# One trunk kernel on one core: addresses of the weight slots, the queue of the general expert path, and the shape of the down products

## The chip, the cores and the metric

The kernel runs on one core of one Trainium2 chip. The metric is the device time of one execution in microseconds (us). The core has five instruction queues that matter here: TensorE (PE, matrix products, with its weight loads shown apart as PEld), VectorE (DVE), ScalarE (ACT), GpSimd (POOL) and SyncE (SP, which here does nothing but start DMAs), and 16 DMA engines that bring weights from HBM into SBUF. Each queue executes its instructions in the order in which they were issued; queues wait for each other through semaphores.

## The reference, cut to what matters

There are 256 tokens of 1024 channels and two layers. Each layer mixes tokens (layer 0 by windowed means, layer 1 by latent attention) and then runs a hierarchical mixture of experts: 4 groups of 8 experts, each token goes to the two best experts of its best group. All numbers are float32.

```python
def hier_moe(h, rg_w, rg_b, re_w, re_b, w_gate, w_up, w_down):
    ...
    gp = jax.nn.softmax((ht @ rg_w + rg_b).astype(jnp.float32), axis=-1)
    g_idx = jnp.argmax(gp, axis=-1)
    ...
    top_p, top_i = lax.top_k(jax.nn.softmax(el, axis=-1), TOP_K)
    gates = g_prob[:, None] * top_p / jnp.sum(top_p, axis=-1, keepdims=True)
    ...
    def expert_block(args):
        xr, e = args
        return (jax.nn.silu(xr @ w_gate[e]) * (xr @ w_up[e])) @ w_down[e]
    ...
    out = jnp.zeros((T, D), jnp.float32).at[row_tok].add(y * row_w[:, None])
```

The 32 experts of a layer have 6 MB of weights each, gate and up 1024 x 512 and down 512 x 1024, and all of them are read whatever the routing says: 192 MB per layer, nearly all of the 419 MB that the kernel moves.

## The kernel before

**Weights and slots.** The host packs all weights into chunks of 1 MB, 128 partitions of 2048 floats. `order` (lines 90 to 95) is the list of chunks as they are needed: one for the pooling mixer, 16 pairs of experts in layer 0 with 12 chunks a pair, 11 for attention, 16 pairs in layer 1. SBUF holds 22 slots of one chunk each (`slot`, line 100). `load` (line 103) takes the next chunk of the list and issues its DMA on SP's queue (line 110). `done` (line 116) says that a chunk has been used, and issues the next load into the slot that comes free; that DMA waits on SP for the last product that reads the slot. So the list is fetched in order, up to 22 chunks ahead.

**Routing.** `route_half` transposes a block of 128 tokens on PE. `route_block` is a generator in three stages. Stage 1 sums the squares, takes `rstd` (two GpSimd operations in `rsqrt`, lines 162 and 163), adds the residual to the output sums with an identity product (line 323), and lets ScalarE form `xh`, the upper part of the normalised tokens. Stage 2 is the router product (line 331). Stage 3 finds the group and the two experts with a chain of small DVE operations (lines 334 to 348, ending in the mask `mb`), forms the lower part `xl` of the tokens with two GpSimd operations per half (lines 351 and 353), and calls `gates`. `route_end` counts tokens per expert with small products against the masks, gives each token its place `pos` (line 381), builds selection matrices `sel` (`prepare`, line 404), sets `flag` when an expert has more than 64 tokens, and gathers the tokens of the first four experts by products with `sel` (`gather`, lines 422 and 424). `warm` issues products whose result isn't used.

**The general path.** `overflow` (lines 529 to 566) is for the case that an expert has more than 64 tokens. All queues read `flag` (line 532) and branch on it (lines 537 and 538); inside is a loop over the 16 pairs whose weight loads are on SP's queue (line 543). It stands at the head of `experts`, so each queue reaches the branch in front of the first pair.

**Experts.** `experts` takes the pairs in order. Two experts share the partitions of PE's output, 64 each (`CAP`). Eight chunks hold gate and up (line 468, products of 512 columns into the PSUM banks `g` and `u`); ACT and DVE form the activation `sg`, PE transposes it (line 486) into `hT`. Four chunks hold the down weights, chunk c the output columns 256c to 256c + 255 with all four 128-row blocks of both experts. Per chunk c, PE makes eight products of 256 columns (line 507), ACT and DVE take the result to SBUF in two float32r parts (lines 511 and 512), and `scatter` adds them with the transposed selection into the sums `acc[c]` (line 497): one PSUM bank per c, with the two token blocks in its halves. The scatter of one chunk is issued behind the products of the next. The last pair of a stage also evicts the sums and starts the following part (`during`).

A float32 product shows as two matmul instructions and two weight loads.

Of the kernel before, what the change touches and what calls it, by code (L numbers as in the profile page):

```python
# [19 lines left out]
P = 128  # L20
# [7 lines left out]
NE = 32  # L28
# [23 lines left out]
def trunk(ctx: ExitStack, tc: tile.TileContext, x_d, w_d, small_d, rows_d, out_d):  # L52
# [102 lines left out]
    V.memset(ones_bf, 1.0)  # L155
    zero_bf = cst.tile([P, P], BF16, name="zero_bf")
    V.memset(zero_bf, 0.0)
    match = cst.tile([P, 2, 8], F32, name="match")
# [122 lines left out]
    def route_start(l):  # L281
        r = Route()
        r.l = l
        r.ss, r.xT = [None] * 2, [None] * 2
        r.rstd = sb([P, 2], f"rstd{l}")
        r.lg = sb([P, 2, 40], "lg")
        r.g8 = sb([P, 2, 8], "g8")
        r.e8 = sb([P, 2, 8], "e8")
        r.el = sb([P, 2, NE], "el")
        r.mb = sb([P, 2, NE], "mb", dt=BF16)  # L290
        r.gw = sb([P, 2, NE], "gw")
        r.pos = sb([P, 2, NE], "pos")

        r.acc = [ps("c") for _ in range(NB)]
        return r

    def warm(n):

        p = ps("u")
        for _ in range(n):  # L300
            T.matmul(p, zero_bf, zero_bf[:, 0:1].to_broadcast([P, 512]), start=True, stop=True)

# [13 lines left out]
    def route_block(r, i):  # L316
# [3 lines left out]
        rsqrt(r.rstd[:, i:i + 1], r.ss[i][:, 0:1], 1.0 / D)  # L320

        for c in range(NB):
            T.matmul(r.acc[c][:, i * 256:(i + 1) * 256], ident, x(i, c * 256, 256),
                     start=i == 0, stop=False, skip_group_check=True)
        for hh in range(2):
            A.mul(xh[:, i, hh * 512:(hh + 1) * 512], xs[i][hh], r.rstd[:, i:i + 1])
        yield
        p = ps("t")
        for k in range(DC):
            c = C_RW + 288 * l + 36 * k  # L330
            T.matmul(p[:, 0:40], r.xT[i][:, k // 4, k % 4 * P:(k % 4 + 1) * P], small[:, c:c + 40], start=k == 0, stop=k == DC - 1)
        yield
        lg, g8, e8, el = r.lg[:, i], r.g8[:, i], r.e8[:, i], r.el[:, i]
# [11 lines left out]
        V.tensor_copy(match[:, 1, 0:2], e8[:, 0:2])  # L345
        t32 = sb([P, NE], "t32")
        V.match_replace(t32, match[:, 1], el, HIT)
        V.tensor_scalar(r.mb[:, i], t32, HIT, None, op0=OP.is_ge)
        for hh in range(2):
# [3 lines left out]
            G.tensor_tensor(xs[i][hh], xx, xh[:, i, hh * 512:(hh + 1) * 512].bitcast(F32), op=OP.subtract)  # L353
        gates(r, i)
        yield

    def gates(r, i):
        nm = sb([P, 2], "nm", bufs=2)
        V.tensor_scalar(nm[:, 0:1], r.e8[:, i, 0:1], -1.0, None, op0=OP.mult)
        V.tensor_scalar(nm[:, 1:2], r.g8[:, i, 0:1], -1.0, None, op0=OP.mult)  # L360
        ex = sb([P, NE], "ex")
# [90 lines left out]
    def experts(r, before_last, during):  # L452
# [4 lines left out]
        for q in range(NPAIR):  # L457
# [35 lines left out]

            def scatter(c, ys=ys, selT=h.selT[:, j], last=last):
                for i in range(2):
                    for n in range(2):
                        T.matmul(r.acc[c][:, i * 256:(i + 1) * 256], selT[:, i], ys[c][:, n], start=False,  # L497
                                 stop=last and n == 1, skip_group_check=True)
                if last:
                    for i in range(2):  # L500
                        evac(c + i, x(i, c * 256, 256), r.acc[c][:, i * 256:(i + 1) * 256])

            for c in range(NB):
                w = chunk(base + 8 + c)
                p = ps("t")
                for f, e in by_expert(base + 8 + c, 4):
                    T.matmul(p[e * CAP:(e + 1) * CAP, 0:256], hT[:, f, e * CAP:(e + 1) * CAP],  # L507
                             w[:, e * 1024 + f * 256:e * 1024 + f * 256 + 256], start=f == 0, stop=f == 3)
                done(base + 8 + c)
                y = sb([P, 2, 256], "y", "b2", dt=F32R)  # L510
                A.copy(y[:, 0], p[:, 0:256])  # L511
                V.tensor_tensor(y[:, 1], p[:, 0:256], y[:, 0].bitcast(F32), op=OP.subtract)  # L512
                ys.append(y)
                if c:
                    scatter(c - 1)
                if last:
                    during(c)
            if last:
                scatter(NB - 1)
                for c in range(NB, NB + 4):  # L520
                    during(c)
            else:
                pend = lambda scatter=scatter: scatter(NB - 1)
            if q == NPAIR - 2:
# [4 lines left out]
    def overflow(r):  # L529

        l = r.l
        v = nc.values_load(r.flag[0:1, 0:1], min_val=0, max_val=1)
        hks = sb([P, 2, P], "hks", "b1")
        w, hs, hT = (sb([P, 512], n, "b2") for n in ("wov", "hso", "hTo"))
        gate = sb([P, 2, 2], "gate")
        g, u, pt = ps("g"), ps("u"), ps("t")
        with tc.If(v > 0):
            with tc.For_i(0, NPAIR, 1) as q:
                V.tensor_copy(gate, r.go[:, :, ds(q * 2, 2)])

                def weights(k, e, n):
                    o = e * 1024 + n * 512
                    nc.sync.dma_start(w, w_d[ds(MOE_CHUNK[l] + k + q * 12, 1), :, o:o + 512].rearrange("o p n -> (o p) n"))

                for e in range(2):
                    for i in range(2):
                        for k in range(DC):
                            for t in (upper_x, x):
                                T.matmul(pt[:, 0:P], t(i, k * P, P).bitcast(F32), ident, start=t is upper_x, stop=t is x)
                            hk = hks[:, k % 2]  # L550
                            V.tensor_scalar(hk, pt[:, 0:P], small[:, C_FFN + 8 * l + k:C_FFN + 8 * l + k + 1], None,
                                            op0=OP.mult)
                            for n, p in enumerate((g, u)):
                                weights(k, e, n)
                                T.matmul(p, hk, w, start=k == 0, stop=k == DC - 1)
                        A.activation(hs, g, AF.Silu)
                        V.scalar_tensor_tensor(hs, hs, gate[:, i, e:e + 1], u, op0=OP.mult, op1=OP.mult)
                        for f in range(4):
                            T.transpose(pt[:, f * P:(f + 1) * P], hs[:, f * P:(f + 1) * P], ident)
                        A.copy(hT, pt)  # L560
                        for c in range(NB):
                            for f in range(4):
                                if f % 2 == 0:
                                    weights(8 + c, e, f // 2)
                                T.matmul(r.acc[c][:, i * 256:(i + 1) * 256], hT[:, f * P:(f + 1) * P],
                                         w[:, f % 2 * 256:(f % 2 + 1) * 256], start=False, stop=False, skip_group_check=True)

# [121 lines left out]
    def attention():  # L689
# [219 lines left out]
        for n in range(4):  # L909
# [40 lines left out]
    stages = [route_block(r, i) for i in range(2)]  # L950
    for _ in range(3):
        for stage in stages:
            next(stage)
    route_end(r)
# [25 lines left out]
def packed(v):  # L980
# [3 lines left out]
    for l in range(2):  # L984
        c = w[MOE_CHUNK[l]:MOE_CHUNK[l] + NPAIR * 12].reshape(NPAIR, 12, P, 2, 2, 512)
        for n, name in enumerate(("w_gate", "w_up")):
            c[:, 0:8, :, :, n] = v[name][l].reshape(NPAIR, 2, 8, P, 512).transpose(0, 2, 3, 1, 4)
        d = w[MOE_CHUNK[l]:MOE_CHUNK[l] + NPAIR * 12].reshape(NPAIR, 12, P, 2, 4, 256)
        d[:, 8:12] = v["w_down"][l].reshape(NPAIR, 2, 4, P, NB, 256).transpose(0, 4, 3, 1, 2, 5)
    a = w[ATT_CHUNK:]  # L990
# [53 lines left out]
```

## Time and profile before

| | us |
|---|---|
| median of 3 runs | 1082.19 |
| lowest and highest | 1081.85, 1083.34 |
| the profiled execution | 1082.35 |
| its span in the trace | 1080.3 |
| PE busy | 1007.9 (93%) |
| DVE, ACT, POOL busy | 255.4, 165.2, 85.1 |

The profile is of one execution. Its times count from the first instruction of the program; the span ends with the last one, and the execution's own time holds 2.05 us more around it. A matmul's end is modelled, so a busy PE isn't a PE at its peak. A row of the timeline has start, duration, engine, line and operation, and in brackets the idle time ahead of it and what ended that. The first expert stage lies between 56 and 508 us, attention and the second routing behind it, the second expert stage between 628 and 1070 us.

### The profile page before, as it was taken

To read this page: it belongs to the slowest core of one execution; us is meant where nothing else is said; L and a number is where in the kernel's file an instruction comes from. 1 tells how busy PE (TensorE), PEld (TensorE's weight loads), DVE (VectorE), ACT (ScalarE), POOL (GpSimd) and SP (SyncE) were. 2 spreads that over 40 slices of the span, in tenths; PEclk is the share of its full clock that TensorE was granted. 3 is DMA by queue.
4 is the path that set the end of the run, shared out by engine and by line. 5 is a ranking of instruction groups with operands and counts; after the bars stand their busy time and mean duration, and the time that the engine had idled before them with its cause. 6 is when DMAs were issued, how large, how long until landed. Compare 5 with 4: busy or idle time off the path is not lost. (4 is left out here: it accounts for less than half of the span.)

```text
span 1080.3 us, 15133 instructions
## 1 busy us (share of the span) xinstructions
PE 1007.9 (93%) x6338; PEld 574.3 (53%) x6338; DVE 255.4 (24%) x543; ACT 165.2 (15%) x413; POOL 85.1 (8%) x88
## 2 busy tenths in 40 slices
PE   6699999999999998989889889999999999999996
PEld 5545555555555543535878645555555555554543
DVE  5502121212121201123775512121212121211102
ACT  4100101010101010024632200101010101010013
POOL 4400000000000000000464400000000000000001
PEclk9889999999999999999999999999999999999999
DMA  9989999999999999999655959999999999999993
GB/s 361 417 352 420 419 418 421 418 419 421 417 419 419 419 420 419 420 420 418 241 229 175 370 224 420 420 418 420 419 419 419 418 420 420 417 420 420 417 417 148
DMA packets 59260, 418.86 MB, mean 388 GB/s; under 512 B 6704, under 2 KB 6704, under 8 KB 9136
## 3 DMA queue, kind: packets, MB, share of 16 engines
q1 hardware_dynamic: 58608, 416.84, 93.7%
q8 instruction: 53, 0.87, 0.3%
q10 hardware_dynamic: 576, 0.96, 0.3%
q14 instruction: 23, 0.19, 0.0%
HBM read 416.72 MB, written 1.05 MB: 387 GB/s over the span
## 5 line engine op out<-in xcount | busy, mean ns | idle before, releaser
L468 PE MATMUL ps_g<-slot,xg 128*64 128x512 f32 x1024 | 274.9, 604 | 24.2 <-DMA slot<-w_in 14.9
L468 PE MATMUL ps_u<-slot,xg 128*64 128x512 f32 x1024 | 270.7, 595 | 0.0
L507 PE MATMUL ps_t<-slot,hT 128*64 128x256 f32 x2048 | 245.1, 384 | 9.2 <-DVE hT L221 8.3
L507 PEld LDWEIGHTS ps_t<-slot,hT 128*64 128x64 f32 x2048 | 140.8, 137 | 84.6 <-DVE hT L221 12.1
L468 PEld LDWEIGHTS ps_u<-slot,xg 128*64 128x64 f32 x1024 | 84.4, 138 | 138.0 <-issue 138.0
L468 PEld LDWEIGHTS ps_g<-slot,xg 128*64 128x64 f32 x1024 | 76.5, 137 | 148.1 <-issue 97.3
L477 DVE SCALAR_TENSOR_TENSOR sg<-sg,gates,ps_u 128x512 f32<-128x512 f32 x32 | 23.9, 747 | 473.1 <-PE ps_u L468 473.1
L512 DVE TENSOR_TENSOR y<-ps_t,y 128x256 fp32r<-128x256 f32 x128 | 54.3, 424 | 242.9 <-ACT y L511 242.9
L497 PEld LDWEIGHTS ps_c<-y,selT 128*128 128x128 f32 x512 | 68.4, 188 | 61.5 <-issue 36.9
L497 PE MATMUL ps_c<-y,selT 128*128 128x256 f32 x512 | 94.5, 306 | 0.1
L511 ACT CAST y<-ps_t 128x256 fp32r<-128x256 f32 x128 | 47.6, 372 | 248.9 <-PE ps_t L507 248.9
L476 ACT ACTIVATE sg<-ps_g 128x512 f32<-128x512 f32 x32 | 19.1, 597 | 409.2 <-PE ps_g L468 393.0
L422 PE MATMUL ps_t<-sel,xh 128*128 128x256 f32 x256 | 54.3, 294 | 0.0
L422 PE MATMUL ps_t<-sel,xl 128*128 128x256 f32 x256 | 52.3, 286 | 0.0
L424 DVE TENSOR_TENSOR xg<-ps_t,small 128x512 f32<-128x512 f32 x64 | 44.2, 691 | 28.7 <-PE ps_t L422 28.7
L422 PEld LDWEIGHTS ps_t<-sel,xh 128*128 128x128 f32 x256 | 40.8, 196 | 1.3 <-issue 1.1
L422 PEld LDWEIGHTS ps_t<-sel,xl 128*128 128x128 f32 x256 | 40.7, 195 | 0.0
L944 POOL TENSOR_TENSOR x<-x,slot 128x256 f32<-128x256 f32 x5 | 3.5, 724 | 450.5 <-ACT junka L942 450.5
L162 POOL TENSOR_SCALAR rstd_a<-acca 128x2 f32<-128x2 f32 x1 | 0.2, 192 | 473.8 <-DVE acca L655 473.8
L619 POOL TENSOR_TENSOR slot<-slot 128x1024 fp32r<-128x1024 f32 x11 | 27.1, 2485 | 3.8 <-PE ps_c L191 3.4
L219 ACT COPY hT<-ps_g 128x256 f32<-128x256 f32 x32 | 11.9, 372 | 64.9 <-DVE hT L221 61.3
L486 PE MATMUL ps_g<-ident,sg 128*128 128x128 f32 x128 | 19.8, 277 | 1.3 <-DVE sg L477 1.3
(263 smaller groups left out, 678.3 us busy)
## 6 DMA issues: line engine op xcount, KB each, us to landing
slot<-w_in SPq DMA_DIRECT2D x391, 1024.0 KB, 19.9
slot<-w_in SPq DMA_DIRECT2D x10, 512.0 KB, 13.3
x<-x_in SPq DMA_DIRECT2D x4, 256.0 KB, 5.4
out<-x SPq DMA_DIRECT2D x2, 256.0 KB, 2.6
out<-x ACTq DMA_DIRECT2D x2, 256.0 KB, 2.6
small<-small_in ACTq DMA_DIRECT2D x1, 388.5 KB, 4.2
rb<-rows_in ACTq DMA_DIRECT2D x1, 40.0 KB, 5.7
```

The costliest lines, as they stand in the source:

```text
L219: A.copy(dst, src)
L422: T.matmul(o, w(i, kk * P, P), h.sel[:, i], start=n == 0, stop=n == 3)
L424: V.tensor_tensor(h.xg[hh][:, 2 * m:2 * m + 2], p.rearrange("p (k s) -> p k s", k=2), small[:, c:c + 2, None].to_broadcast([P, 2, 4 * CAP] ...
L468: T.matmul((g, u)[n][e * CAP:(e + 1) * CAP], h.xg[k // 4][:, k % 4, s0 + e * CAP:s0 + (e + 1) * CAP], w[:, e * 1024 + n * 512:e * 1024 + n ...
L476: A.activation(sg, g, AF.Silu)
L477: V.scalar_tensor_tensor(sg, sg, h.gate[:, j:j + 1], u, op0=OP.mult, op1=OP.mult)
L486: T.transpose(pt[:, f * P:(f + 1) * P], sg[:, f * P:(f + 1) * P], ident)
L497: T.matmul(r.acc[c][:, i * 256:(i + 1) * 256], selT[:, i], ys[c][:, n], start=False, stop=last and n == 1, skip_group_check=True)
L507: T.matmul(p[e * CAP:(e + 1) * CAP, 0:256], hT[:, f, e * CAP:(e + 1) * CAP], w[:, e * 1024 + f * 256:e * 1024 + f * 256 + 256], start=f == ...
L511: A.copy(y[:, 0], p[:, 0:256])
L512: V.tensor_tensor(y[:, 1], p[:, 0:256], y[:, 0].bitcast(F32), op=OP.subtract)
L619: eng.tensor_tensor(lo, w, hi.bitcast(F32), op=OP.subtract)
```

## The change

- **Down products.** Except in the last pair of a stage, the four down chunks of a pair are packed anew: output half n (512 columns) takes chunks 8 + 2n and 9 + 2n, each with two of the four row blocks of both experts. PE makes products of 512 columns, eight calls per chunk become four, and the result is taken to SBUF in two operations of 512 columns per half.
- **Sums.** They are held as `acc[i][hh]`, by token block i and half hh of the columns, one bank each. The identity product of the residual is two calls of 512 columns per block instead of four of 256. `scatter` adds 512 columns at once, the first half's behind the first chunk of the second half, the second half's in the next pair.
- **Routing order.** The router product stands ahead of the identity product. The lower part of the tokens moves out of `route_block` into `lower_x` and from four GpSimd operations per block to two DVE operations. `gates` moves out of `route_block` into `route_end`, behind `prepare`.
- **General path.** Its weight loads go to GpSimd's queue. The loops are now over pair and expert, once for all pairs but the last and once for the last, whose down chunks keep the old packing; the two token parts are added on DVE in front of the transpose.
- **SBUF.** GpSimd's DMAs need scratch memory, which lies at the start of SBUF and grows from 16 to 512 bytes per partition. All tiles behind it move, the slots with them. To make room, `zero_bf` goes (`warm` uses `tri`) and `t32` and `ex` share a buffer.

```diff
-        for c in range(NB):
-            T.matmul(r.acc[c][:, i * 256:(i + 1) * 256], ident, x(i, c * 256, 256),
-                     start=i == 0, stop=False, skip_group_check=True)
-        for hh in range(2):
-            A.mul(xh[:, i, hh * 512:(hh + 1) * 512], xs[i][hh], r.rstd[:, i:i + 1])
-        yield
         p = ps("t")
         for k in range(DC):
...
+        for hh in range(2):
+            A.mul(xh[:, i, hh * 512:(hh + 1) * 512], xs[i][hh], r.rstd[:, i:i + 1])
+
+        for hh in range(2):
+            T.matmul(r.acc[i][hh], ident, xs[i][hh], start=True, stop=False, skip_group_check=True)
         yield
...
+    def lower_x(r, i):
+
         for hh in range(2):
             xx = xs[i][hh]
-            G.tensor_scalar(xx, xx, r.rstd[:, i:i + 1], None, op0=OP.mult)
             xs[i][hh] = tokens("xl", F32R)
-            G.tensor_tensor(xs[i][hh], xx, xh[:, i, hh * 512:(hh + 1) * 512].bitcast(F32), op=OP.subtract)
-        gates(r, i)
-        yield
+            V.scalar_tensor_tensor(xs[i][hh], xx, r.rstd[:, i:i + 1], xh[:, i, hh * 512:(hh + 1) * 512].bitcast(F32),
+                                   op0=OP.mult, op1=OP.subtract)
...
         r.first = prepare(r, 0)
+        for i in range(2):
+            gates(r, i)
...
+                for n in range(2):
+                    p = ps("t")
+                    for f in range(4):
+                        w = chunk(base + 8 + 2 * n + f // 2)
+                        for e in range(2):
+                            o = e * 1024 + f % 2 * 512
+                            T.matmul(p[e * CAP:(e + 1) * CAP], hT[:, f, e * CAP:(e + 1) * CAP], w[:, o:o + 512],
+                                     start=f == 0, stop=f == 3)
+                        if f % 2:
+                            done(base + 8 + 2 * n + f // 2)
+                            if n == 1 and f == 1:
+                                scatter(0, 512)
+                    ys += [two_parts(p, 512), None]
+                pend = lambda scatter=scatter: scatter(2, 512)
...
-                    nc.sync.dma_start(w, w_d[ds(MOE_CHUNK[l] + k + q * 12, 1), :, o:o + 512].rearrange("o p n -> (o p) n"))
...
+                        G.dma_start(w, w_d[ds(MOE_CHUNK[l] + k + q * 12, 1), :, ds(e * 1024 + n * 512, 512)]
+                                    .rearrange("o p n -> (o p) n"))
...
         out_proj(1, [ps("g"), ps("u")], {(0, 0): lambda: next(stages), (0, 1): lambda: next(stages),
-                                         (0, 3): lambda: next(stages), (1, 2): lambda: route_half(r, 1, 0)})
+                                         (0, 3): lambda: lower_x(r, 0), (1, 2): lambda: route_half(r, 1, 0)})
         route_half(r, 1, 1)
         list(route_block(r, 1))
+        lower_x(r, 1)
         route_end(r)
...
-    nc = bacc.Bacc("TRN2", target_bir_lowering=False, num_devices=1, dynamic_dma_scratch_size=16)
+    nc = bacc.Bacc("TRN2", target_bir_lowering=False, num_devices=1, dynamic_dma_scratch_size=512)
```

More of the change, by code (lines that the diff above doesn't have):

```diff
@@ L155, in trunk @@
     V.memset(ones_bf, 1.0)
-    zero_bf = cst.tile([P, P], BF16, name="zero_bf")
-    V.memset(zero_bf, 0.0)
     match = cst.tile([P, 2, 8], F32, name="match")
@@ L292, in route_start @@
         r.pos = sb([P, 2, NE], "pos")
-        r.acc = [ps("c") for _ in range(NB)]
+        r.acc = [[ps("c") for _ in range(2)] for _ in range(2)]
         return r
@@ L300, in warm @@
         for _ in range(n):
-            T.matmul(p, zero_bf, zero_bf[:, 0:1].to_broadcast([P, 512]), start=True, stop=True)
+            T.matmul(p, tri, tri[:, 0:1].to_broadcast([P, 512]), start=True, stop=True)
     def route_half(r, i, hh):
@@ L360, in gates @@
         V.tensor_scalar(nm[:, 1:2], r.g8[:, i, 0:1], -1.0, None, op0=OP.mult)
-        ex = sb([P, NE], "ex")
+        ex = sb([P, NE], "ex", "row", 1)
         A.activation(ex, r.el[:, i], AF.Exp, bias=nm[:, 0:1])
@@ L492, in experts, with scatter @@
             ys = []
-            def scatter(c, ys=ys, selT=h.selT[:, j], last=last):
+            def scatter(c, n, ys=ys, selT=h.selT[:, j], last=last):
                 for i in range(2):
-                    for n in range(2):
-                        T.matmul(r.acc[c][:, i * 256:(i + 1) * 256], selT[:, i], ys[c][:, n], start=False,
-                                 stop=last and n == 1, skip_group_check=True)
+                    o = r.acc[i][c // 2][:, c % 2 * 256:c % 2 * 256 + n]
+                    for m, y in enumerate(ys[c]):
+                        T.matmul(o, selT[:, i], y, start=False, stop=last and m == 1, skip_group_check=True)
@@ L499, in scatter @@
                 if last:
                     for i in range(2):
[L501 to L516, printed above, removed]
+                        evac(c + i, x(i, c * 256, 256), r.acc[i][c // 2][:, c % 2 * 256:(c % 2 + 1) * 256])
@@ new lines, in two_parts @@
+            def two_parts(p, n):
+                hi, lo = (sb([P, n], "y", "b2", dt=F32R) for _ in range(2))
+                A.copy(hi, p)
+                V.tensor_tensor(lo, p, hi.bitcast(F32), op=OP.subtract)
+                return hi, lo
+            if last:
+                for c in range(NB):
+                    w = chunk(base + 8 + c)
+                    p = ps("t")
+                    for f, e in by_expert(base + 8 + c, 4):
+                        T.matmul(p[e * CAP:(e + 1) * CAP, 0:256], hT[:, f, e * CAP:(e + 1) * CAP],
+                                 w[:, e * 1024 + f * 256:e * 1024 + f * 256 + 256], start=f == 0, stop=f == 3)
+                    done(base + 8 + c)
+                    ys.append(two_parts(p[:, 0:256], 256))
+                    if c:
+                        scatter(c - 1, 256)
@@ L517, in experts @@
                     during(c)
-            if last:
-                scatter(NB - 1)
+                scatter(NB - 1, 256)
                 for c in range(NB, NB + 4):
@@ L532, in overflow, with weights @@
         v = nc.values_load(r.flag[0:1, 0:1], min_val=0, max_val=1)
-        hks = sb([P, 2, P], "hks", "b1")
+        sums, hk = (sb([P, P], n, "b1") for n in ("sums", "hk"))
         w, hs, hT = (sb([P, 512], n, "b2") for n in ("wov", "hso", "hTo"))
-        gate = sb([P, 2, 2], "gate")
+        gate = sb([P, 2, 1], "gate")
         g, u, pt = ps("g"), ps("u"), ps("t")
         with tc.If(v > 0):
[L538 to L542, printed above, removed]
-                    nc.sync.dma_start(w, w_d[ds(MOE_CHUNK[l] + k + q * 12, 1), :, o:o + 512].rearrange("o p n -> (o p) n"))
-                for e in range(2):
+            for last in range(2):
+                with tc.For_i(last * (NPAIR - 1), NPAIR - 1 + last, 1) as q, tc.For_i(0, 2, 1) as e:
+                    V.tensor_copy(gate, r.go[:, :, ds(q * 2 + e, 1)])
+                    def weights(k, n):
+                        G.dma_start(w, w_d[ds(MOE_CHUNK[l] + k + q * 12, 1), :, ds(e * 1024 + n * 512, 512)]
+                                    .rearrange("o p n -> (o p) n"))
                     for i in range(2):
                         for k in range(DC):
-                            for t in (upper_x, x):
-                                T.matmul(pt[:, 0:P], t(i, k * P, P).bitcast(F32), ident, start=t is upper_x, stop=t is x)
-                            hk = hks[:, k % 2]
+                            V.tensor_tensor(sums, upper_x(i, k * P, P).bitcast(F32), x(i, k * P, P).bitcast(F32), op=OP.add)
+                            T.transpose(pt[:, 0:P], sums, ident)
                             V.tensor_scalar(hk, pt[:, 0:P], small[:, C_FFN + 8 * l + k:C_FFN + 8 * l + k + 1], None,
@@ L561, in overflow @@
                         for c in range(NB):
[L562 to L566, printed above, removed]
+                            for m in range(2):
+                                weights(8 + c, m)
+                                for f, a, b in [(2 * m + k, c * 256, k * 256) for k in range(2)] if last else \
+                                        [(c % 2 * 2 + m, c // 2 * 512, 0)]:
+                                    n = 256 if last else 512
+                                    T.matmul(r.acc[i][a // 512][:, a % 512:a % 512 + n], hT[:, f * P:(f + 1) * P],
+                                             w[:, b:b + n], start=False, stop=False, skip_group_check=True)
     aw = [ATT_CHUNK + n for n in range(11)]
@@ L950, in trunk @@
     stages = [route_block(r, i) for i in range(2)]
-    for _ in range(3):
-        for stage in stages:
-            next(stage)
+    for stage in stages:
+        next(stage)
+    for i in range(2):
+        lower_x(r, i)
+    for stage in stages:
+        next(stage)
     route_end(r)
@@ L987, in packed @@
             c[:, 0:8, :, :, n] = v[name][l].reshape(NPAIR, 2, 8, P, 512).transpose(0, 2, 3, 1, 4)
-        d = w[MOE_CHUNK[l]:MOE_CHUNK[l] + NPAIR * 12].reshape(NPAIR, 12, P, 2, 4, 256)
-        d[:, 8:12] = v["w_down"][l].reshape(NPAIR, 2, 4, P, NB, 256).transpose(0, 4, 3, 1, 2, 5)
+        down = v["w_down"][l]
+        c[:-1, 8:12] = down[:-2].reshape(NPAIR - 1, 2, 2, 2, P, 2, 512).transpose(0, 5, 2, 4, 1, 3, 6) \
+            .reshape(NPAIR - 1, 4, P, 2, 2, 512)
+        c[-1, 8:12] = down[-2:].reshape(2, 4, P, NB, 256).transpose(3, 2, 0, 1, 4).reshape(4, P, 2, 2, 512)
     a = w[ATT_CHUNK:]
```

9 lines of the change are left out of this document (5 added, 4 removed).

## The prediction

> **What bounds the kernel now.** I read the page's slices first: which resource is full, stage by stage.
>
> ```profile
> span 1080.3 us, 15133 instructions
> DMA  9989999999999999999655959999999999999993
> GB/s 361 417 352 420 419 418 421 418 419 421 417 419 419 419 420 419 420 420 418 241 229 175 370 224 420 420 418 420 419 419 419 418 420 420 417 420 420 417 417 148
> ```
>
> A slice is 27 us. Both expert stages (slices 3 to 18, 24 to 38) move 417 to 421 GB/s with the DMA engines full: TensorE (PE), 93% busy, is not the limit there. Bytes are lost in three places: slice 2 (352), slices 19 to 23 (attention and the second routing), and the start and end. A gain can only come from those places, or from the rate. The first hole, in windows of 5 us (after the engines' busy times: granted clock, DMA share, GB/s):
>
> ```profile
> 60.00:65.00 5.00, 5.00 (x27) 2.08 (x28) 0.00 (x0) 0.16 (x1) 0.00 (x0) 0.88 0.97 401
> 65.00:70.00 5.00, 5.00 (x26) 1.98 (x24) 0.00 (x0) 0.00 (x0) 0.00 (x0) 1.00 0.26 70
> 70.00:75.00 5.00, 4.15 (x24) 1.70 (x20) 1.17 (x2) 1.18 (x2) 0.00 (x0) 1.00 1.02 428
> ```
>
> Against 420 GB/s this lacks (19 + 350) x 5 / 420 = **4.4 us** of transfer. Why, show the line of the branch around the general path (window 40 to 80), the waits of SP's queue there, SP's and PE's timelines:
>
> ```profile
> L537 SPq EVENT_SEMAPHORE  x8: 17/17/17, 57.7 to 67.9; - x8
> L537 SPq COMPARE_BRANCH  x1: 45/45/45, 48.2 to 48.2; - x1
> SPq L537 <- SPq L537: 19.5, 5, 9.5
> 68.03 5.22 SPq L110 DMA_DIRECT2D slot<-w_in  x8
> 57.59 1.95 PE L468 MATMUL ps_u<-slot,xg 128*64 128x512 f32 x4
> ```
>
> SP branches at 48.2 and then executes eight semaphore instructions, the last at 67.9; its next load leaves at 68.03, though PE had finished chunk 0 near 59.5. Eight waits over 10.2 us are one per 2.5 us at most, the time of one 1 MB load at 420 GB/s: SP is waiting for its own loads in flight, and the rings run dry. The line has the loads of the general path; its untaken side must bring SP's load semaphores level.
>
> That hole reaches the end, for the first expert stage ends at DMA's pace:
>
> ```profile
> 488.89 1.08 PE L468 MATMUL ps_g<-slot,xg 128*64 128x512 f32 x4 [0.55 <-DMA slot<-w_in]
> 491.38 1.08 PE L468 MATMUL ps_g<-slot,xg 128*64 128x512 f32 x4 [0.55 <-DMA slot<-w_in]
> ```
>
> The second hole (windows) ends when PE frees the first slot of the second stage; all slots are full before, and from there DMA is the bound to the end:
>
> ```profile
> 625.00:630.00 5.00, 2.04 (x6) 0.86 (x8) 0.37 (x1) 0.00 (x0) 0.00 (x0) 0.78 0.02 3
> 630.00:635.00 5.00, 5.00 (x36) 2.24 (x34) 0.00 (x0) 0.16 (x1) 0.00 (x0) 0.88 0.41 157
> 1060.00:1065.00 5.00, 5.00 (x35) 3.37 (x32) 1.19 (x3) 1.92 (x7) 0.78 (x2) 1.00 0.24 93
> ```
>
> So every microsecond by which the second stage starts earlier is a microsecond of the total.
>
> **The change part by part.** *General path on GpSimd's queue.* No load of the general path is among the page's DMA issues, so its body does not run and its new loops cost nothing. What changes is who waits at the branch: SP issues no DMA in there any more and should pass it at once; GpSimd takes the semaphore work, with no load of its own in flight. If it stood there 10 us as SP does, nothing would be late, since its next work comes 473.8 us on:
>
> ```profile
> L162 POOL TENSOR_SCALAR rstd_a<-acca 128x2 f32<-128x2 f32 x1 | 0.2, 192 | 473.8 <-DVE acca L655 473.8
> ```
>
> SP then issues at chunk 0's release (59.5 or earlier) while loads in flight last until 67.7: -4.4 us. Bounds: 0 (SP still waits) and -4.4, all that the hole holds; I take -4.4.
>
> *Second routing.* PE, DVE and POOL timelines, and DVE's of the first routing (the two rows at 34 us):
>
> ```profile
> 609.21 1.89 PE L323 MATMUL ps_c<-x,ident 128*128 128x256 f32 x8
> 610.93 1.88 PE L331 MATMUL ps_t<-small,xT 128*128 128x40 f32 x16
> 610.60 0.57 POOL L163 TENSOR_TENSOR rstd<-rstd,half 128x1 f32<-128x1 f32 x1
> 612.91 0.26 DVE L334 SCALAR_TENSOR_TENSOR lg<-ps_t,rstd,rb 128x40 f32<-128x40 f32 x1 [2.68 <-PE ps_t L331]
> 613.86 1.10 DVE L340 TENSOR_SCALAR t<-t 128x4 f32<-128x4 f32 x1
> 615.00 0.65 DVE L341 TENSOR_TENSOR el<-lg,t 128x32 f32<-128x32 f32 x1
> 616.57 1.26 POOL L353 TENSOR_TENSOR xl<-x,xh 128x512 fp32r<-128x512 f32 x1
> 616.83 1.04 DVE L348 TENSOR_SCALAR mb<-t 128x32 bf16<-128x32 f32 x1
> 617.78 0.14 DVE L359 TENSOR_SCALAR nm<-e 128x1 f32<-128x1 f32 x1
> 619.16 0.21 DVE L381 SCALAR_TENSOR_TENSOR pos<-mb,ps_t 128x64 f32<-128x64 bf16 x1
> 619.41 0.76 DVE L404 TENSOR_TENSOR sel<-slot_no,pos 128x256 fp32r<-128x256 f32 x2
> 34.40 0.17 DVE L340 TENSOR_SCALAR t<-t 128x4 f32<-128x4 f32 x1
> 34.61 0.19 DVE L341 TENSOR_TENSOR el<-lg,t 128x32 f32<-128x32 f32 x1
> 624.25 0.40 PE L422 MATMUL ps_t<-sel,xl 128*128 128x256 f32 x2
> 627.96 1.98 PE L468 MATMUL ps_g<-slot,xg 128*64 128x512 f32 x4 [3.32 <-PEq L537]
> L537 PEldq COMPARE_BRANCH  x2: 3772/4900/6028, 49.5 to 623.9; - x2
> L477 DVE SCALAR_TENSOR_TENSOR sg<-sg,gates,ps_u 128x512 f32<-128x512 f32 x32 | 23.9, 747 | 473.1 <-PE ps_u L468 473.1
> ```
>
> (a) The router's products move ahead of the identity products (L323, 1.72 us from its start to L331's). Then lg waits no longer for PE's queue but for rstd, which POOL ends at 611.17, and that end itself comes some 0.3 earlier because DVE no longer works on gates when the residual sum needs it: lg near 611.0, 1.9 us earlier.
> (b) DVE's chain from lg to mb takes 612.91 to 617.87. L348 ends 0.04 us after POOL's L353 (617.83): DVE stood behind GpSimd. With GpSimd's four operations gone, L340 and L341 cost as at 34 us (0.17 and 0.19), L348 some 0.2 as its nearest small row does: -0.93, -0.46 and -0.84; with the copies between them about -2.5.
> (c) Now DVE does the lower part: two operations per block, of two SBUF inputs and 512 columns; no such row exists. Nearest is L477 (0.75), bounds 0.38 (one half of L404's row) and 1.26 (L353): 1.5 us for both, before pos. Against it the gates leave that place: 617.78 to 619.16 = 1.38. Net 0.
> (d) What is late next: both gates now stand between sel and the flag on DVE, 2 x 1.38. Behind them on DVE wait the count's maximum, which frees the PSUM buffer that the second gather tile needs, and the four evictions of the gather. With sel ready near 615.3, the gates end at 618.3, maximum, flag and r.go at 618.9, the first eviction at 619.6; the fourth tile starts near 620.6, against 623.5 before. So of some 4.5 us won at sel, **2.9** are left.
> (e) The branch comes behind the last tile and costs PE 3.77 us here (6.03 in the first routing). The skipped body is shorter, but still several hundred PE instructions: I keep 3.77; bounds 0.05 (as SP) and 6.03.
> Value -2.9; bounds: -0.6 (branch as the long one) and -4.6 (the gates hide, as the gather's own products do now) to -6.6 (the branch gets short too). The block of rows 0 gains the same on DVE under the output projection's products: covered, 0. The first routing gets some 5 us shorter; covered by 22 loaded slots, 0.
>
> *Down products.* The chain's rows (16 products of 256 columns; 4 of 512) give the cost:
>
> ```profile
> 650.47 1.88 PE ps_t L507 x16
> 640.59 0.86 PE ps_g L468 x4
> ```
>
> Per chunk 16 x 0.1175 becomes 8 x 0.215 = 1.72, -0.16; per pair -0.64, and the sums (half as many, twice as wide) about as much again. Up to 1.3 us per pair, 39 us in 30 pairs, all covered: DMA feeds a pair of 12 MB in 30 us whatever PE does. If DMA were faster, this would be the reserve. Evictions grow from 256 to 512 columns, half as many, with 2.5 us of room per chunk. Worth 0. The last pair of each stage keeps its form, so the tail after the last load stays.
>
> **Sum.** Execution 1082.35 (span 1080.3 and 2.05 around it), median of the runs shown 1082.19. 1082.35 - 4.4 - 2.9 = 1075.05; from the median 1074.9. I say **1075**.
>
> **The rivals.**
> *SP still waits* (chance 0.06): another reason than the body's loads ties SP to the eight waits. Only the routing counts: 1082.35 - 2.9 = 1079.4. Against: the other engines execute no such row of eight, and SP alone issues DMAs in the body.
> *The routing wins nothing* (0.12): gates and evictions fill DVE, or the branch takes 6.03. Then 1082.35 - 4.4 - 0.6 = 1077.3 or a little more. For it: (d) has DVE full from 611 to 620.
> *The slots' move makes packets cheaper* (0.16). The DMA scratch grows from 16 to 512 bytes, and with it every tile moves up: by the tiles' sizes in the code, slots start at byte 22528 instead of 22048 of a partition, 22528 being 44 x 512. If a write that starts off such a boundary costs more, the 35 full slices, 945 us, get shorter: by 1% 9.5 us, 1065.5; by 3% 28, 1047. For it: nothing is seen, since all loads of before go to slots of one alignment. Against: the rate has one value, 417 to 421, with no second kind of packet.
> [...]
> *The move makes packets dearer* (0.05), the slower side: same place, other sign, should the new start put the loads' writes in step with each other or with PE's reads. It decides from a loss of 7.3 / 945 = 0.8% of the rate (below 416 GB/s in the full slices); at 2%, 1082.35 - 7.3 + 19 = 1094. Against: full slices now spread by 1% only.
> *Neither term comes* (0.05): 1082.
>
> **How the numbers follow.** Forecast 0.56: 1072 to 1077. With the lost routing (0.12) and the rival of SP (0.06) above it, and the smaller prices of cheaper packets (0.06 of its 0.16, down to 1.1%) below it, 1064 to 1080 holds 0.80. Measurement tells about 0.2% from no change, 2.2 us: faster (below 1080.0) is forecast, lost routing, cheaper packets and most of SP's rival, 0.88 with two thirds of the last; same 0.06; slower 0.06.
>
> **What would show it.** Right: SP's next load after the branch leaves right behind chunk 0, no window under 400 GB/s from 60 to 75; the first stage ends 4.4 us earlier; mb costs 0.2 us; PE's first gate product of the second stage is 7.3 us earlier; the rate stays 417 to 421. Wrong: eight waits still on SP; a rate other than 420; PE waiting for something other than a load late in the stages; DVE's gates holding the gather longer than 3 us.

## The result and the profile after

| | before | after |
|---|---|---|
| median (lowest to highest), us | 1082.02 (1081.04 to 1083.34), 4 runs | 1054.95 (1054.34 to 1055.81), 4 runs |
| the profiled execution, us | 1082.35 | 1055.81 |
| its span, us | 1080.3 | 1054.1 |

The ratio is 0.975, with a 95% interval of 0.9733 to 0.9766. The change saves 27.1 us where 7.3 were forecast, and the time lies below the range of 1064 to 1080. The page's head, and its rows by slices of 26.4 us, are the first thing to read.

```profile
span 1054.1 us, 12501 instructions
...
PE 984.4 (93%) x5122; PEld 485.2 (46%) x5122; DVE 243.5 (23%) x490; ACT 156.0 (15%) x353; POOL 62.5 (6%) x72
...
DMA  9999999999999999999655869999999999999994
GB/s 357 425 424 427 426 427 426 427 427 427 426 427 426 428 427 427 427 426 427 269 211 191 367 265 426 426 426 427 427 427 427 426 427 427 426 427 427 427 424 161
```

Two things are new. Slice 2 no longer dips (424, it was 352), as forecast. And every full slice moves 424 to 428 GB/s instead of 417 to 421, which was forecast not to happen. The hole by windows (engines' busy times, granted clock, DMA share, GB/s), and the line of the branch on each queue (duration in ns as least/median/most, first and last start):

```profile
60.00:65.00 5.00, 5.00 (x24) 1.94 (x24) 0.00 (x0) 0.16 (x1) 0.00 (x0) 0.98 1.02 429
65.00:70.00 5.00, 5.00 (x26) 1.97 (x24) 0.00 (x0) 0.00 (x0) 0.00 (x0) 1.00 1.01 421
70.00:75.00 5.00, 4.15 (x24) 1.72 (x22) 1.17 (x2) 1.55 (x3) 0.00 (x0) 1.00 1.01 426
```

```profile
L553 POOLq EVENT_SEMAPHORE  x8: 17/43/43, 51.7 to 608.3; - x8
...
L553 SPq COMPARE_BRANCH  x2: 45/49/53, 48.0 to 605.6; - x2
L553 PEldq COMPARE_BRANCH  x2: 3292/4530/5768, 49.4 to 607.3; - x2
L553 DVEq COMPARE_BRANCH  x2: 72/72/72, 51.5 to 609.5; - x2
L553 DVEq EVENT_SEMAPHORE  x2: 21/21/21, 52.1 to 612.4; - x2
```

SP keeps its branch and has no semaphore row any more; GpSimd has four at each branch, eight in all, and nothing behind it is late. The hole is gone.

The second routing, from VectorE's timeline and then TensorE's (start, duration, engine, line, operation, idle time ahead):

```profile
596.57 0.26 DVE L330 SCALAR_TENSOR_TENSOR lg<-ps_t,rstd,rb 128x40 f32<-128x40 f32 x1 [1.31 <-PE ps_t L322]
...
597.52 0.17 DVE L336 TENSOR_SCALAR t<-t 128x4 f32<-128x4 f32 x1
597.72 0.19 DVE L337 TENSOR_TENSOR el<-lg,t 128x32 f32<-128x32 f32 x1
...
598.67 0.18 DVE L344 TENSOR_SCALAR mb<-t 128x32 bf16<-128x32 f32 x1
598.76 1.63 DVE L352 SCALAR_TENSOR_TENSOR xl<-x,rstd,xh 128x512 fp32r<-128x512 f32 x2
600.84 0.22 DVE L379 SCALAR_TENSOR_TENSOR pos<-mb,ps_t 128x64 f32<-128x64 bf16 x1 [0.45 <-PE ps_t L378]
601.10 0.76 DVE L404 TENSOR_TENSOR sel<-slot_no,pos 128x256 fp32r<-128x256 f32 x2
```

```profile
604.88 0.47 PE L422 MATMUL ps_t<-sel,xh 128*128 128x256 f32 x2 [1.81 <-DVE most L385]
...
610.90 1.08 PE L468 MATMUL ps_g<-slot,xg 128*64 128x512 f32 x4 [1.79 <-PEq L553]
612.47 1.08 PE L468 MATMUL ps_u<-slot,xg 128*64 128x512 f32 x4 [0.50 <-DVEq L553]
```

The mask takes 0.18 us as forecast, and the gather's second tile stands behind the gates (step (d)). The first gate product of the second stage starts at 610.90, 17.1 us earlier than before. The other 9 us of the span are won behind it, in the second expert stage itself.

### The profile page after: what moved, and what is told of

It reads as the page before. It is cut to its first block, busy times and chain, and to the rows that moved or that the text cites. A ratio compares the mean times of both kernels' runs of the same rounds, so it can differ in the third digit from the quotient of the medians.

```text
span 1054.1 us, 12501 instructions
## 1 busy us (share of the span) xinstructions
PE 984.4 (93%) x5122; PEld 485.2 (46%) x5122; DVE 243.5 (23%) x490; ACT 156.0 (15%) x353; POOL 62.5 (6%) x72
## 3 DMA queue, kind: packets, MB, share of 16 engines
HBM read 416.72 MB, written 1.05 MB: 396 GB/s over the span
## 5 line engine op out<-in xcount | busy, mean ns | idle before, releaser
L532 PE MATMUL ps_t<-slot,hT 128*64 128x512 f32 x960 | 219.2, 598 | 8.3 <-DVE hT L219 8.3
L532 PEld LDWEIGHTS ps_t<-slot,hT 128*64 128x64 f32 x960 | 63.6, 136 | 127.6 <-issue 112.3
L507 DVE TENSOR_TENSOR y<-ps_t,y 128x512 fp32r<-128x512 f32 (+1 forms) x68 | 44.9, 660 | 255.6 <-ACT y L506 248.0
L499 PE MATMUL ps_c<-y,selT 128*128 128x512 f32 (+1 forms) x272 | 77.7, 407 | 0.7 <-DVE x L219 0.7
L476 ACT ACTIVATE sg<-ps_g 128x512 f32<-128x512 f32 x32 | 19.1, 597 | 398.5 <-PE ps_g L468 383.3
L506 ACT CAST y<-ps_t 128x512 fp32r<-128x512 f32 (+1 forms) x68 | 38.1, 560 | 251.2 <-PE ps_t L532 237.7
L499 PEld LDWEIGHTS ps_c<-y,selT 128*128 128x128 f32 x272 | 44.8, 188 | 57.1 <-issue 26.6
L422 PE MATMUL ps_t<-sel,xl 128*128 128x256 f32 x256 | 52.5, 288 | 0.0
L636 POOL TENSOR_TENSOR slot<-slot 128x1024 fp32r<-128x1024 f32 x11 | 27.1, 2482 | 4.4 <-PE ps_c L189 3.4
L188 PE MATMUL ps_c<-slot 128*128 128x256 f32 (+2 forms) x62 | 19.2, 309 | 1.1 <-DVE slot L182 1.1
```

Of the source, the lines that this page charges most:

```text
L188: T.matmul(o, a.hi, b.lo, start=False, stop=False)
L422: T.matmul(o, w(i, kk * P, P), h.sel[:, i], start=n == 0, stop=n == 3)
L476: A.activation(sg, g, AF.Silu)
L499: T.matmul(o, selT[:, i], y, start=False, stop=last and m == 1, skip_group_check=True)
L506: A.copy(hi, p)
L507: V.tensor_tensor(lo, p, hi.bitcast(F32), op=OP.subtract)
```

## The experiments

The first theory after the result: the slots' new start sets the rate (16 us), the hole gives 4.4, the rest is routing, and the down products give nothing. The rival: the rate comes from the rest of the change.

**The slots' start.** Five kernels differ in where the slots begin. Two put unused bytes in front of them (the kernel before gives up `zero_bf` for the room and shares a buffer between `t32` and `ex`, as the change does), three change the size of the scratch alone.

```diff
     xh = cst.tile([P, 2, D], F32R, name="xh")
+    cst.tile([P, 8], F32, name="pad")      # the change, slots at 22560
...
+    cst.tile([P, 120], F32, name="pad")    # before, slots at 22528
...
-dynamic_dma_scratch_size=512
+dynamic_dma_scratch_size=256               # the change; also 448 and 384
```

> The changed kernel with 32 unused bytes in front of the weight slots, so that these start at byte 22560 (32 beyond a multiple of 512) instead of 22528 (a multiple of 512). Theory 'the slots' start sets the rate': the full slices fall back from 424-428 to 417-421 GB/s, the common packet from 309 to 313-320 ns, and about 1.7% of some 945 us, 16 us, comes back: 1071 us (1068 to 1074). Rival 'the rate comes from the rest of the change' (wider down products, SP's queue that no longer drains): 1055 us and 424-428 GB/s as with the change.

> The kernel before with nothing changed but the place of the slots (480 unused bytes, room made by giving up the tile of zeros and sharing one small buffer): slots at byte 22528. Theory 'the slots' start sets the rate': 424-428 GB/s in the full slices and 16 us less than before, 1066 us (1063 to 1069), with the hole at 64 to 69 us still there. Rival 'the rest of the change': 1082 us, 417-421 GB/s.

> The changed kernel with the DMA scratch at 256 instead of 512 bytes: slots at byte 22272, a multiple of 256 but not of 512. Theory 'the slots' start sets the rate', if 64, 128 or 256 bytes is the unit that counts: 1055 us and 424-428 GB/s. If 512 is the unit: 1071 us. Rival 'the rest of the change': 1055 us here too, so this run only separates the units.

> The changed kernel with a DMA scratch of 448 bytes: slots at byte 22464, a multiple of 64 but not of 128. Theory 'the slots' start sets the rate': if the unit is 64 bytes, 1055 us; if it is 128 or more, about 1071 us and 417-421 GB/s. Rival 'the rest of the change': 1055 us.

> The changed kernel with a DMA scratch of 384 bytes: slots at byte 22400, a multiple of 128 but not of 256. If the unit of the slots' start is 128 bytes: 1055 us, packets of 309 ns. If it is 256 bytes (as multiples of 256 had 1055 and 64 beyond one 1068): 1068 us, packets of 309 to 320 ns.

The packet times below are the mean over the trace's 50048 packets of 8192 bytes (one partition's row of a chunk).

| kernel | slots' first byte | beyond a multiple of 256 | packet, ns | median, us |
|---|---|---|---|---|
| before | 22048 | 32 | 316.7 | 1082.0 |
| before, slots moved | 22528 | 0 | 310.8 | 1067.5 |
| the change | 22528 | 0 | 311.2 | 1055.0 |
| scratch 256 | 22272 | 0 | 311.1 | 1054.9 |
| scratch 384 | 22400 | 128 | 315.4 | 1067.5 |
| scratch 448 | 22464 | 192 | 315.5 | 1068.2 |
| the change, 32 bytes on | 22560 | 32 | 316.2 | 1071.0 |

The page's rate rows of the change with 32 bytes more, and of the kernel before with slots moved:

```profile
GB/s 355 417 417 419 418 419 420 420 419 420 419 420 418 421 420 419 420 418 420 279 232 174 376 282 419 418 419 420 419 421 419 420 419 419 419 419 421 418 417 171
```

```profile
GB/s 362 425 356 426 427 427 426 427 426 426 427 426 427 426 426 427 427 426 426 230 227 180 373 238 426 427 426 427 427 426 426 426 427 426 425 427 427 426 423 119
```

The start alone switches the rate of the full slices, in both directions: the change falls from 424-428 GB/s to 417-421, and the kernel before rises from 417-421 to 423-427. The rival is out. The start 128 bytes beyond a multiple of 256 has nearly the slow price (315.4 ns a packet), the starts on a multiple the full rate (310.8 to 311.2), also 22272, which is no multiple of 512. Of 64, 128, 256 and 512 bytes only 256 fits the starts tried here. In the kernel before, the move alone is worth 14.5 us (ratio 0.9863, 0.9847 to 0.988), three quarters of the 19.8 us that the change saves beyond the forecast.

**The general path alone.** On top of the moved slots, the weight loads of the general path go to GpSimd's queue, and nothing else.

```diff
-                    nc.sync.dma_start(w, w_d[ds(MOE_CHUNK[l] + k + q * 12, 1), :, o:o + 512].rearrange("o p n -> (o p) n"))
+                    G.dma_start(w, w_d[ds(MOE_CHUNK[l] + k + q * 12, 1), :, o:o + 512].rearrange("o p n -> (o p) n"))
```

> The kernel before with slots at byte 22528 (as the run that only moved them, 1067.5 us) and the general path's weight loads on GpSimd's queue; routing order, down products and sums as before. Theory 'the hole': SP passes the branch at once, no window from 60 to 75 us lacks transfer, and the (56 + 306) x 5 / 426 = 4.25 us that the hole holds with moved slots come off the total: 1063.3 us (1062.3 to 1064.3). Rival 'the hole is refilled later anyway' or SP waits for another reason: 1067.5 us.

Measured: 1062.74 us (1060.46 to 1063.66), 4.8 less. The windows of this run are full where the hole was:

```profile
60.00:65.00 5.00, 5.00 (x33) 2.30 (x33) 0.00 (x0) 0.16 (x1) 0.00 (x0) 0.83 1.00 421
65.00:70.00 5.00, 5.00 (x26) 1.94 (x24) 0.00 (x0) 0.00 (x0) 0.00 (x0) 1.00 1.02 431
```

**With the routing order, without the down products.** The routing part of the diff shown above is added; `acc`, `scatter` and the packing stay as before.

```diff
+    def lower_x(r, i):
...
         r.first = prepare(r, 0)
+        for i in range(2):
+            gates(r, i)
```

> As the run before it in this list, and the routing order of the change (router ahead of the identity products, lower part on VectorE, gates behind the first selection matrices); down products and sums as before. It is the change without its down products. Theory 'down products are worth nothing' (PE waits for loads in every pair): 1055 us, as the change, with all the rest of the gain, 8 us, from the routing. Rival 'the wider down products help' (shorter way from the first gate product to the first free slots, or less traffic in PSUM and SBUF): 1058 to 1061 us, the routing being worth 2.9 to 5 us.

Measured: 1059.97 us (1057.20 to 1060.62). By the medians the routing is worth 2.8, and my theory falls: the rest of the change, the down products with their sums, which this kernel lacks, is worth the 5.0 us to 1054.95. What TensorE waited for from 640 to 1030 us shows why; the rows give what was waited for, then us in total, times and the longest. In order: before, this kernel, the change.

```profile
PE ps_g L468 <- DMA slot<-w_in: 1.2, 2, 0.6
```

```profile
PE ps_t L509 <- DVE hT L219: 3.6, 7, 0.5
```

```profile
PE ps_g L468 <- DMA slot<-w_in: 6.2, 13, 0.7
PE ps_t L532 <- DVE hT L219: 3.6, 7, 0.5
```

This kernel has no wait for a load there at all, and seven short ones for `hT`. TensorE works almost without a pause (3.6 us of waits in 390), so its own time is the bound. Before the change it hardly waited for loads there either: two waits, 1.2 us. Its pace can be read from a small product that comes once in two pairs, in the first pair's first chunk. The first and the last of the second stage, without and with the new down products:

```profile
615.41 1.02 PE L434 MATMUL ps_t<-gw,sel 128*64 128x1 f32 x16
...
994.41 0.63 PE L434 MATMUL ps_t<-gw,sel 128*64 128x1 f32 x16
```

```profile
613.38 0.63 PE L432 MATMUL ps_t<-gw,sel 128*64 128x1 f32 x16
...
985.46 0.63 PE L432 MATMUL ps_t<-gw,sel 128*64 128x1 f32 x16
```

The seven steps between them, from the same rows:

| kernel | seven steps of two pairs, us |
|---|---|
| before | 54.1 54.1 54.1 54.1 54.1 54.5 55.3 |
| without new down products | 55.1 54.0 54.0 54.0 54.0 54.0 54.0 |
| the change | 52.0 52.4 52.5 52.4 52.4 52.4 58.0 |

A step that waits for nothing takes 54.0 with the old down products and 52.4 with the new ones, 0.8 per pair. The loads of two pairs take 24 x 1.0486 MB / 426 GB/s = 59.1 us, and yet TensorE isn't held until the last step, because the stage starts with 22 loaded slots.

**More work on TensorE.** If that is so, work added to TensorE must move the end. Four products without a use go into each of 15 pairs of the second stage, once without and once with the new down products.

```diff
+                if l == 1 and k == 4 and not last:
+                    warm(4, "t")
```

> The change without its down products (1060.0 us in the run above), and in each of the first 15 pairs of the second expert stage four more bf16 products of 512 columns on TensorE whose result isn't used; nothing reads or waits for them. By the row of such products (three in 0.81 us) they add some 0.9 us to a pair, 14 us to the stage. Theory 'TensorE works off its backlog to the very end': its two-pair step of 54.0 us is not held by any load, so the end moves by all of it, 1073 us (1071 to 1075). Rival 'the loads set the end of the stage': 1060 us, at most 1062.

> The changed kernel with the same added products. Its two-pair step of 52.4 us becomes about 54.3, that of the run without the new down products (54.0). Theory 'TensorE works off its backlog': the first 1.6 us per two pairs had been what brought the loads back as the bound, so the added products take back what the down products gave, 1059 to 1062 us. Rival 'the loads set the end': 1055 us.

Measured: 1074.72 us (1074.26 to 1077.72), 14.7 more, and 1064.67 us (1062.09 to 1066.46), 9.7 more. The steps become 56.2 and 54.6, so the products cost 1.1 per pair, not 0.9. Without the new down products nearly all of 15 x 1.1 = 16.5 shows. With them, the waits for loads that the change had in this stage are gone, and so part of the work costs nothing: by the traces the seven steps are 11.2 longer together (383.3 against 372.1), the stretch behind them is 2.9 shorter, and the first row stands 1.1 later, 9.4 in all. My expectation for this one was too low, since it took the work at 0.9 and the start as equal; the theory stands, the rival (1055) doesn't.

**The forecast's own kernel.** General path and routing, old down products, slots 32 bytes beyond a multiple of 256: this is what the forecast's terms describe. The edit to the kernel without the new down products:

```diff
     xh = cst.tile([P, 2, D], F32R, name="xh")
+    cst.tile([P, 8], F32, name="pad")
```

> The change without its down products and with slots 32 bytes beyond a multiple of 256, as before: what the prediction on record holds for likeliest (general path and routing win, rate as before, down products worth nothing). The prediction's sum: 1075 us. Theory 'the down products pay only where the loads are fast enough': at 418-420 GB/s loads hold TensorE back at the end of the stage, so the down products are worth little here, within 1.5 us of the run with all of the change on such slots (1071.0 us, spread 1068.5 to 1072.9): 1070 to 1072.5. Rival 'the down products shorten TensorE's way whatever the rate': 1075 to 1076.

Measured: 1073.51 us (1072.17 to 1074.90). It lies between the two expectations. Against the whole change on such slots (1071.0, 1068.5 to 1072.9, on another chip) the down products are worth some 2.5 us here, with spreads that overlap; by the medians half of the 5.0 at 427 GB/s, but whether it is 1 us or 4 stays open. In the two profiled runs they are worth 4.4 (spans of 1071.2 and 1066.8, the second being the fastest of its four runs), about as much as at 427 GB/s (4.8). So it isn't shown that they pay less at the slower rate.

**The lower part back on GpSimd.**

```diff
-            V.scalar_tensor_tensor(xs[i][hh], xx, r.rstd[:, i:i + 1], xh[:, i, hh * 512:(hh + 1) * 512].bitcast(F32), op0=OP.mult, op1=OP.subtract)
+            G.tensor_scalar(xx, xx, r.rstd[:, i:i + 1], None, op0=OP.mult)
+            G.tensor_tensor(xs[i][hh], xx, xh[:, i, hh * 512:(hh + 1) * 512].bitcast(F32), op=OP.subtract)
```

> The changed kernel with the lower part of the tokens back on GpSimd (two operations per half, as before), at its new place in the order. Theory 'VectorE stands behind GpSimd' (step (b) of the prediction): in the second routing four GpSimd operations of about 1.2 us come back and slow the small VectorE operations beside them; 1.5 to 3 us later, 1056.5 to 1058 us. Rival 'the gates set the end whatever the lower part does' or GpSimd runs beside VectorE at no cost: 1055 us.

Measured: 1057.20 us (1055.78 to 1058.20), 2.25 more. VectorE's timeline has the slow small operations again:

```profile
596.54 0.58 DVE L337 TENSOR_TENSOR el<-lg,t 128x32 f32<-128x32 f32 x1
...
598.31 1.04 DVE L344 TENSOR_SCALAR mb<-t 128x32 bf16<-128x32 f32 x1
```

0.58 against 0.19, and 1.04 against 0.18, beside GpSimd's operations of 1.3 to 1.6 us. The ratios to before, 0.977 (0.9754 to 0.9787) and 0.975 for the change, have intervals that overlap: the slower operations are shown more surely than the 2.25.

**Gates between the gather's tiles.** In the change the second tile waits 1.81 us for a maximum that stands behind both gates. Here maximum and flag come first.

```diff
-        for i in range(2):
-            gates(r, i)
         most = sb([P, 1], "most")
...
         warm(WARM[1])
-        for hh in range(2):
-            gather(r, r.first, hh)
+        gates(r, 0)
+        gather(r, r.first, 0)
+        gates(r, 1)
...
+        gather(r, r.first, 1)
```

> The changed kernel with the maximum and the flag in front of the gates, the first block's gates in front of the first two gather tiles' evictions and the second block's behind them. In the changed kernel TensorE stands 1.81 us in the gather for the maximum behind both gates. Theory 'the second routing is on the path until its last product, and VectorE's order sets it': the gather ends 1.4 to 1.8 us earlier and so does everything behind it, 1053.3 us (1053 to 1054). Rival 'VectorE has the same work in another order' and its branch comes no earlier: 1055 us.

Measured: 1052.59 us (1052.51 to 1054.39), ratio to before 0.9736 (0.972 to 0.9753). Behind its first products the gather waits only 0.18, for an eviction, and the stage's first row stands at 607.59, 3.3 us earlier than in the profile of the change:

```profile
602.43 0.50 PE L422 MATMUL ps_t<-sel,xh 128*128 128x256 f32 x2 [0.18 <-DVE xg L424]
...
607.59 1.50 PE L468 MATMUL ps_g<-slot,xg 128*64 128x512 f32 x4 [3.06 <-PEq L553]
```

Not all of the 3.3 is this edit's: the profile of the change has its selection matrices 1.75 later to begin with and slower products in the gather. The run with a scratch of 256, whose routing is that of the change, has its matrices at the same time as this run (599.31 and 599.35) and its first row at 609.13: 1.5 later, within the forecast 1.4 to 1.8. At the medians this run is 2.4 us faster than the change; the two ratios come from different chips and their intervals overlap, so the size is less sure than the removed wait.

## Why the prediction was wrong, step by step

| step | forecast, us | measured alone, us |
|---|---|---|
| rate (slots' start) | 0 | -14.5 |
| hole (general path) | -4.4 | -4.8 |
| second routing | -2.9 | -2.8 |
| down products | 0 | -5.0 |

The last column is the ladder of medians 1082.0, 1067.5, 1062.7, 1060.0, 1055.0. Its rungs are 3 to 15 us and the runs of one kernel spread by 1 to 3.5; the kernels ran on different chips, and by their ratios to the before that was measured with each, the rungs are 14.8, 4.3, 3.4 and 4.5.

The traces show where each rung lies. The first stage's last rows of gate and up products, in the order of the ladder without the routing's (479.60):

```profile
492.29 1.03 PE L468 MATMUL ps_u<-slot,xg 128*64 128x512 f32 x4
```

```profile
484.27 1.03 PE L467 MATMUL ps_u<-slot,xg 128*64 128x512 f32 x4
```

```profile
479.66 1.03 PE L466 MATMUL ps_u<-slot,xg 128*64 128x512 f32 x4
```

```profile
479.55 1.03 PE L468 MATMUL ps_u<-slot,xg 128*64 128x512 f32 x4
```

| kernel | that row, us | second stage's first gate row, us | from there to the end of the span, us |
|---|---|---|---|
| before | 492.29 | 627.96 | 452.3 |
| slots moved | 484.27 | 619.26 | 446.3 |
| general path too | 479.66 | 614.62 | 446.1 |
| routing too | 479.60 | 611.97 | 446.9 |
| the change | 479.55 | 610.90 | 443.2 |
| routing too, slots 32 bytes on | 487.65 | 620.39 | 450.8 |
| the change, slots 32 bytes on | 487.84 | 618.70 | 448.1 |

The loads set the end of the first stage: only the slots' start (8.0) and the hole (4.6) move it, and the shorter down products don't (479.60 and 479.55). The routing's 2.6 lies between the stages. The share of the down products in the second stage is 3.7 at 427 GB/s, some 1 of it from a low clock at the start of the one run (its first step of 55.1 above), and 2.7 at the slower rate. Another 1.0 and 1.9 lie ahead of that stage, where the identity products and the skipped body changed with them; no run separates these.

**Hole: right.** SP stood at its eight semaphore rows until 67.9 us, by their pace for its own loads (an estimate from eight rows in 10.2 us). In the change the eight rows are GpSimd's, with 17 to 43 ns each and nothing behind them. The first stage ends 4.6 us earlier for it.

**Routing: right in the sum, and mostly in its parts.** The rows of VectorE in the kernel with only slots and general path changed:

```profile
599.51 0.26 DVE L332 SCALAR_TENSOR_TENSOR lg<-ps_t,rstd,rb 128x40 f32<-128x40 f32 x1 [2.68 <-PE ps_t L329]
...
600.46 1.10 DVE L338 TENSOR_SCALAR t<-t 128x4 f32<-128x4 f32 x1
...
603.42 1.04 DVE L346 TENSOR_SCALAR mb<-t 128x32 bf16<-128x32 f32 x1
```

(a) lg's wait for the router shrinks from 2.68 to 1.31, 1.4 where 1.9 was forecast; lg still waits for the router's products, not for rstd as forecast. (b) From lg to the end of mb 4.95 us become 2.28: 2.7, forecast 2.5. (c) The lower part takes 1.63, forecast 1.5. (d) The gates do hold the gather, by 1.81. (e) TensorE's branch at the second routing takes 3.29 us instead of 3.77. A cost that was not forecast: VectorE passes its branch at 609.5 and its next row stands at 612.4, and so TensorE's second product of the stage waits 0.5 for it. On (b) the run with the lower part back on GpSimd has the slow rows again: the mask takes 1.04 against 0.18 beside GpSimd's operations. In what way GpSimd's operations slow them no run shows.

**Rate: wrong, and the largest error.** The failing step is the choice of the likeliest case, "the rate stays 417 to 421". The rival "the slots' move makes packets cheaper" had the cause, the bytes and a price of 1% to 3%; 5.5 / 316.7 = 1.7% is what the packets show. It was given 0.16, against it only "the rate has one value, 417 to 421, with no second kind of packet". That was no evidence: all slots of before start equally far beyond a multiple of 256, so one rate is what both cases lead to. Nor do the packets of before have one time: of 50048, 26205 took 313 ns, 8387 took 320 and 6459 took 309; of those of after 49656 took 309. The slices average this away, and the prediction argued from the slices. Its 945 us are too many as well: slices 0, 2 and 22 (361, 352 and 370 GB/s) count among the 35, and 32 slices, 864 us, ran at the full rate; 1.7% of these is 15 us, close to the 14.5.

The unit of 256 bytes rests on the table of starts above. What the runs moved is the side that is written, and the packets that start off a multiple of 256 took 1.4% to 1.8% more than 311.0 ns, those 128 and 192 bytes beyond it (315.4 and 315.5) a little less than those 32 bytes beyond it (316.2 and 316.7). What happens inside the DMA engine no run shows.

**Down products: wrong.** The failing step is "all covered: DMA feeds a pair of 12 MB in 30 us whatever PE does", and with it "from there DMA is the bound to the end". Over the average pair it is true that TensorE needs less time (27.0 us) than the loads (29.55), and in the first stage, whose end the loads set, the term is indeed nothing. But TensorE starts the second stage with 22 loaded slots and has to catch up with that lead before any load can hold it. Its first wait for a load stands 13.4 pairs behind the stage's first small product (631.32) before the change, and 12.4 (from 613.38) with it:

```profile
993.62 1.08 PE L468 MATMUL ps_g<-slot,xg 128*64 128x512 f32 x4 [0.64 <-DMA slot<-w_in]
```

```profile
938.85 1.08 PE L468 MATMUL ps_g<-slot,xg 128*64 128x512 f32 x4 [0.36 <-DMA slot<-w_in]
```

There it gained 30.0 - 27.05 = 2.95 us a pair, and here 29.55 - 26.2 = 3.35: 40 and 42. So the lead is some 40 us, an estimate from these two rows. At 427 GB/s the old down products gain 2.55 a pair, 38 in the 15 pairs ahead of the last: they just miss it, and TensorE is the bound of the whole second stage. The new ones reach it in the last steps, where the 6.2 us of waits stand. The prediction's "up to 1.3 us per pair" measured 0.8. The step was nearly wrong for the kernel before already: its waits for loads from 640 to 1030 us sum to 1.2, and moving its slots won 6.0 in the second stage (452.3 to 446.3), behind which no wait for a load is left there. The two wrong steps hang together: the faster loads alone would have moved the bound to TensorE, and the shorter products moved it back. The prediction called the down products "the reserve" if DMA were faster, and then gave the case of faster packets no such term.

## What to carry to other kernels

Look at where the destination of a stream of DMAs starts before weighing anything else: in this kernel a tile of 480 bytes in front of the slots was worth 14.5 us, more than all rewritten instructions together (4.8 + 2.8 + 5.0 = 12.6). "DMA is busy all the time" didn't make it the bound of the second stage, where 22 loaded slots lay ahead; count how many units the consumer needs to use up that lead. Here it was 12.4 to 13.4 of 16 pairs, and with the faster loads the old down products gained 38 of some 40 us (estimates from the rows above): both sides were within a few us of being the bound. When one term of a sum changes which side is the bound, the terms that were costed at nothing have to be costed again under it: the down products, forecast at 0, measured 5.0.

## What was not expected of the hardware

- In these runs a row of 8192 bytes that starts 32, 128 or 192 bytes beyond a multiple of 256 in an SBUF partition took 315.4 to 316.7 ns on average, one on a multiple of 256 took 310.8 to 311.2; half rows of 4096 bytes took 162.5 (before) and 159.0 (the change).
- TensorE's granted clock was low for a few us somewhere between the gather and the start of the second stage, not at the same place in these two profiles. In the run without the new down products the start of the stage has these windows, and four products took 1.98 us at 611.97 and 1.05 from 617.89 on. In the profile of the change the clock was 1.00 from 610 to 630 us, but 0.66 from 605 to 610, where the gather's pairs of products took 0.63 us instead of 0.40. What share of the spread between runs it has is not shown.

```profile
610.00:615.00 5.00, 3.03 (x8) 1.09 (x9) 0.00 (x0) 0.00 (x0) 0.00 (x0) 0.60 0.02 5
615.00:620.00 5.00, 5.00 (x32) 2.27 (x31) 0.00 (x0) 0.16 (x1) 0.00 (x0) 0.72 0.73 220
```
